# Products of probabilities and values of two sub-blocks issued back to back, every second step, in both attention mixers

## The chip, the cores and the metric

The kernel runs on one core of one Trainium2 chip. The time is that of the whole program on the device, in microseconds; a run's number here is the time of that one core. Of the kernel before, three runs were timed, and one further execution was taken with the hardware profiler.

## What is computed

Two layers of an encoder trunk on 512 tokens of 1024 channels. Each layer has one wide input projection that feeds two attention mixers, two gates, and then an output projection with a layer norm:

```python
u = x * (1.0 + scale) + shift                    # scale, shift, gate from c
aq, ak, av, az, bq, bk, bv, bz, gl = split(u @ w_in)
y_a = mixer_a(aq, ak, av, rel_table) * silu(az)  # 3 groups x 8 heads, windows, relative bias
y_b = mixer_b(bq, bk, bv, q_norm_g, k_norm_g) * silu(bz)   # 8 q heads, 2 kv heads, rms norm, rope
merged = g_a * (y_a @ w_pa) + g_b * (y_b @ w_pb)
x = layer_norm(ALPHA * x + gate * (merged @ w_o))
...
# both mixers, block by block
logits = einsum('qe,ke->qk', q, k) * scale (+ bias, masked)
p = exp(logits - max)
o = einsum('qk,ke->qe', p, v) / sum(p)
```

The change touches the last of these lines, the product of probabilities and values, in both mixers, and only the moment at which it is issued.

## The kernel before, in words

The order of the work is written out by hand: each engine executes its instructions in the order in which the Python code emits them, and semaphores hold an instruction until what it reads is there, or until what it overwrites has been read. TensorE (PE), VectorE (DVE), ScalarE (ACT), GpSimd (POOL) and the DMA queue of SyncE (SP) each have one such order.

**Main and fill.** `weave` (L854) runs two generators against each other. The main one is attention: `mixer_b` and then `mixer_a` for each half of the heads. The fill is the wide projection, `half_chunks` and `z_chunks`, in units of 12 products with 512 columns or 24 with 256 (rows `b<-uh,wh`, `b<-ul,wh`, `b<-uh,wl` and `b<-wh,uh`, `b<-wl,uh`, `b<-wh,ul`: weights and activations are split into a high and a low part, three products for each). Every `yield 1` of the main lets 1.1 fill units through on average. After each unit, `tick` (L340) splits the next piece of weights (`wh` on ACT in L175, `wl` on DVE in L176) and, in layer 0 above all, adds up pieces of the adaLN projection on DVE (`ada_dve`, L281 and L283).

**A sub-block** is 128 queries of two heads and all their keys. `pipeline` (L668) takes them through four stages. `L(i)` makes the logits in the PSUM tile `L`, and the softmax on DVE and ACT leaves the probabilities in the tile `s` (mixer B: maximum L631, exponential L637, scaling by the inverse sum L641; mixer A: bias and maximum L731, exponential L738). `T(i)` transposes them on PE, eight transposes into the PSUM tile `T` (L663), and ACT copies them to `pt` (L665). `V(i)` is the product with the values: eight products, `pt` against 64 columns of values each, that alternate between the upper and lower 64 columns of the array. A row of the profile shows each as two, so that one `V(i)` is 16 records `b<-pt,g 128*64`; all other stationary operands in these stretches have 128 columns. `Q(i)` (mixer B only, L613) transposes the queries two steps ahead.

**One step** of `pipeline` emits `T(i)`, `Q(i+2)`, `L(i+1)`, then a fill slot, then `V(i)`, then another fill slot. There are 16 steps in mixer B and 8 in each half of mixer A, for two layers 64 steps in all. In mixer B, DVE copies the result of each `V(i)` out of PSUM (L655). In mixer A two sub-blocks share one PSUM bank, and ACT copies it out after the second (L773).

**PSUM banks.** `B1` (L60, `Slots`) hands out four banks of one kind, `b`, first freed, first used, to the fill, `Q`, `V` and the sums of the adaLN projection (`ada_sum`, L296: one product with a tile of ones, read by DVE in L301 or L306). A bank counts as free when the code that reads it has been emitted; on the chip the next writer waits for that reader.

Of the kernel before, what the change touches and what calls it, by code (L numbers as in the profile page):

```python
# [38 lines left out]
def trunk_kernel(ctx, tc, x, c, rel_table, ln_g, ln_b, w_ada, b_ada, w_in, b_gate,  # L39
# [565 lines left out]
    def mixer_b(st, ys):  # L605
# [41 lines left out]
        def V(i):  # L647
# [8 lines left out]
            B1.put(o)  # L656

        yield from pipeline(len(subs), Q, L, T, V, lambda i: True, st["more"])

    def transpose_p(p):  # L660
# [7 lines left out]
    def pipeline(n, Q, L, T, V, need, more=()):  # L668
        if Q:
            Q(0)  # L670
            if n > 1:
                Q(1)
        yield 1
        while not need(0):
            yield "need"
        L(0)
        for _ in range(3 if Q else 2):
            yield 1
        for i in range(n):
            T(i)  # L680
            if Q and i + 2 < n:
                Q(i + 2)
            if i + 1 < n:
                while not need(i + 1):
                    yield "need"
                L(i + 1)
            yield 1
            V(i)
            if more:
                more.popleft()()  # L690
            yield 1
# [5 lines left out]
    def mixer_a(st, hf, ys, more=()):  # L697
# [90 lines left out]
        def need(i):  # L788
            k, pr, pp = subs[i]
            return all(("k", g, hf, pr) in st for g in ((1, 2) if k else (0,)))  # L790

        yield from pipeline(len(subs), None, L, T, V, need, more)
        for h in range(4):
            G.put(st.pop(("b0", hf, h)))
# [603 lines left out]
```

## Time and profile before

| what | value |
|---|---|
| median of three runs | 1199.09 us (1197.3 to 1199.76) |
| profiled execution, its own time | 1199.13 us |
| its span in the profile | 1197.0 us, so 2.1 us lie around it |
| mean granted clock of TensorE | 0.995 of full speed |
| busy share of PE, DVE, ACT, POOL | 97%, 56%, 44%, 5% |
| stretches with attention and fill | about 87 to 412 us (layer 0) and 665 to 988 us (layer 1) |

An engine's busy time counts each moment in which at least one of its instructions runs. Products on PE are pipelined: a record of 0.39 us may start every 0.23 us, so the distance from one start to the next tells what a product costs, not its length.

### The profile page before, as it was taken

The page shows a single profiled execution, that of the slowest core. Times are in us where ns is not written, and L with a number is a line of the kernel's source. Part 1 is how long each engine was busy: PE and PEld are TensorE (multiplying, and loading weights), DVE is VectorE, ACT ScalarE, POOL GpSimd, SP SyncE. Part 2 cuts the span into 40 slices and gives each one's busy share as a digit, 9 for nine tenths or more (in the row PEclk, how much of TensorE's full clock was granted, in tenths as well). Part 3 has the DMA queues.
Part 4 walks back from the last instruction along what each step waited for, and adds up shares of the span by engine and source line. Part 5 has one row for each costly group of instructions (what it writes and reads, how often), then busy time and mean ns, then how long its engine had stood idle before and what let it go on. Part 6 is the DMA issues. An engine that isn't in the chain of part 4 may idle for free.

```text
span 1197.0 us, 19187 instructions
## 1 busy us (share of the span) xinstructions
PE 1163.0 (97%) x7491; PEld 998.2 (83%) x7491; DVE 675.4 (56%) x1582; ACT 531.1 (44%) x1112; POOL 54.0 (5%) x85
## 2 busy tenths in 40 slices
PE   7899999999999999999989999999999999999996
PEld 6888888888887787888989888888878778888896
DVE  6776766655455365336755667664333533843477
ACT  2364544444554454323275545544554553533320
POOL 0021000001000000000002001000000000000000
PEclk9999999999999999999999999999999999999998
DMA  9935433546343243334522326335232223323331
GB/s 280 294 116 150 123 109 117 150 133 185 103 128 120 59 129 96 90 104 150 170 71 71 114 91 182 112 107 167 83 114 85 88 73 114 116 88 106 123 107 71
DMA packets 161314, 146.31 MB, mean 122 GB/s; under 512 B 8942, under 2 KB 149078, under 8 KB 161224
## 3 DMA queue, kind: packets, MB, share of 16 engines
q1 hardware_dynamic: 159176, 139.71, 38.5%
q0 software_dynamic: 2048, 5.38, 1.9%
q8 instruction: 59, 0.97, 0.3%
q14 instruction: 31, 0.25, 0.1%
HBM read 134.87 MB, written 8.62 MB: 120 GB/s over the span
## 4 chain that ended last, share of the span: by engine, by line
PE 88%; DVE 6%; ACT 2%; DMA 1%; issue 1%; SPq 1%; POOL 0%; DVEq 0%; ACTq 0%
PE b L90 75%; PE L L90 6%; PE T L663 5%; DVE acc L283 1%; PE T L90 1%; DMA raw<-in_w_ada_dram 1%; PE b L613 1%; DVE wl L176 1%; ACT g L948 0%; DMA s<-in_w_in_dram 0%; SPq L999 0%; DVE g L1252 0%; DVE g L1258 0%; ACT g L1271 0%; DVE wl L1023 0%
## 5 line engine op out<-in xcount | busy, mean ns | idle before, releaser
L176 DVE TENSOR_TENSOR wl<-raw,wh 128x512 fp32r<-128x512 f32 x304 | 205.1, 687 | 286.1 <-ACT wh L175 286.1
L90 PE MATMUL b<-uh,wh 128*128 128x512 f32 x768 | 308.4, 402 | 0.6 <-ACT g L423 0.6
L90 PE MATMUL b<-uh,wl 128*128 128x512 f32 x768 | 299.5, 390 | 1.7 <-DVE wl L176 1.7
L90 PE MATMUL b<-ul,wh 128*128 128x512 f32 x768 | 300.0, 391 | 0.0
L175 ACT ACTIVATE wh<-raw 128x512 fp32r<-128x512 f32 x304 | 179.9, 622 | 32.7 <-issue 24.8
L90 PEld LDWEIGHTS b<-uh,wh 128*128 128x128 f32 x768 | 144.0, 188 | 43.6 <-issue 12.0
L90 PEld LDWEIGHTS b<-uh,wl 128*128 128x128 f32 x768 | 144.2, 188 | 33.8 <-DVE wl L176 2.5
L90 PEld LDWEIGHTS b<-ul,wh 128*128 128x128 f32 x768 | 144.3, 188 | 27.6
L90 PE MATMUL b<-wh,uh 128*128 128x256 f32 x416 | 120.8, 290 | 0.0
L90 PE MATMUL b<-wl,uh 128*128 128x256 f32 x416 | 117.7, 283 | 0.0
L90 PE MATMUL b<-wh,ul 128*128 128x256 f32 x416 | 117.6, 283 | 0.0
L665 ACT ACTIVATE pt<-T 128x1024 f32<-128x1024 f32 x64 | 65.4, 1022 | 73.3 <-PE T L663 70.3
L738 ACT ACTIVATE s<-s,ast 128x256 f32<-128x256 f32 x128 | 63.5, 497 | 68.3 <-DVE ast L733 62.9
L283 DVE SCALAR_TENSOR_TENSOR acc<-raw,sc,acc 128x256 f32<-128x256 f32 x168 | 81.3, 484 | 8.4 <-DMA raw<-in_w_ada_dram 3.2
L90 PEld LDWEIGHTS b<-wh,uh 128*128 128x128 f32 x416 | 79.5, 191 | 4.8 <-issue 3.6
L90 PEld LDWEIGHTS b<-wl,uh 128*128 128x128 f32 x416 | 79.5, 191 | 0.8 <-DVE wl L176 0.2
L90 PEld LDWEIGHTS b<-wh,ul 128*128 128x128 f32 x416 | 79.4, 191 | 0.0
L90 PE MATMUL b<-g,wh 128*128 128x512 f32 x256 | 79.2, 391 | 0.0
L637 ACT ACTIVATE s<-L,bst,qn 128x512 f32<-128x512 f32 x64 | 49.2, 773 | 65.9 <-DVE bst L634 65.9
L90 PE MATMUL b<-wh,g 128*128 128x256 f32 x384 | 71.4, 284 | 0.7 <-DVE g L1191 0.5
L90 PE MATMUL b<-pt,g 128*64 128x128 f32 x1024 | 70.0, 279 | 0.0
L90 PEld LDWEIGHTS b<-pt,g 128*64 128x64 f32 x1024 | 54.6, 136 | 17.7 <-issue 13.7
(177 smaller groups left out, 1615.5 us busy)
## 6 DMA issues: line engine op xcount, KB each, us to landing
raw<-in_w_in_dram SPq DMA_DIRECT2D x126, 512.0 KB, 4.1
raw<-in_w_ada_dram SPq DMA_DIRECT2D x96, 256.0 KB, 3.9
raw<-in_w_o_dram SPq DMA_DIRECT2D x16, 512.0 KB
g<-in_x_dram SPq DMA_DIRECT2D x16, 256.0 KB, 5.5
vph<-g SPq DMA_DIRECT2D x16, 256.0 KB, 2.1
g<-vph SPq DMA_DIRECT2D x16, 256.0 KB, 6.0
g<-frow SPq DMA_DIRECT2D x32, 128.0 KB, 3.1
raw<-in_w_pa_dram SPq DMA_DIRECT2D x8, 512.0 KB, 3.5
```

Source lines behind the costliest of these rows:

```text
L90: pe.matmul(o, l, r, start=start, stop=stop, skip_group_check=True)
L175: act.activation(hi[:, d], raw[:, s], AF.Copy)
L176: dve.tensor_sub(lo[:, d], raw[:, s], hi[:, d].bitcast(F32))
L283: dve.scalar_tensor_tensor(a, raw[:, k], col, a, op0=MUL, op1=ADD)
L613: pe.transpose(o[:, 128 * e:128 * e + 128], qd[:, 2 * (hp % 2) + e], idn)
L637: act.activation(p[:, 512 * e:512 * e + 512], lg[:, 512 * e:512 * e + 512], AF.Exp, scale=f[:, e:e + 1], bias=sm[:, 0, e:e + 1], accum_out ...
L663: pe.transpose(t[:, 128 * j:128 * j + 128], p[:, 128 * j:128 * j + 128], idn)
L665: act.activation(pt, t, AF.Copy)
L738: act.activation(p4[:, e, b], p4[:, e, b], AF.Exp, bias=sm[:, e, b:b + 1], accum_out=s_t[:, rb, e, 1:2])
```

## The change

In `pipeline` the call `V(i)` becomes a pair on odd steps; even steps have none.

```diff
             yield 1
-            V(i)
+            if i % 2:
+                V(i - 1)
+                V(i)
             if more:
                 more.popleft()()
             yield 1
```

All numbers of steps are even, so every `V` is still issued. On PE 32 of the 64 `V` are emitted one step later, directly ahead of the next one; every other PE instruction keeps its place among the rest. On DVE the 16 copies L655 of even sub-blocks move behind with them. The orders of ACT, POOL and SP are the same, row by row. Two tiles `pt` exist before and after, and the pair uses both.

The TensorE order of layer 0, mixer B, steps 6 and 7, before (`T_`, `s_` and `pt_` belong to one sub-block each, `uh,wh` rows stand for a fill unit, `acc,ones` is the sum of a gate piece; the names' numbers count tiles, not banks):

```order
L663 MATMUL T_1642<-idn,s_1582 128x128 x8
L613 MATMUL b_1653<-idn,g_1434 128x128 x2
L90 MATMUL L_1659<-g_842,qst_1571 128x512 x4
L90 MATMUL b_1673<-uh,wh_1518 128x512
...
L90 MATMUL b_1714<-pt_1651,g_720 64x128 x8
L90 MATMUL b_1733<-uh,wh_1518 128x512
...
L663 MATMUL T_1748<-idn,s_1667 128x128 x8
...
L90 MATMUL b_1793<-acc_1634,ones 128x256
L90 MATMUL b_1801<-pt_1757,g_720 64x128 x8
L90 MATMUL b_1811<-wh_1686,uh 128x256
```

The same place on TensorE with the change:

```order
L663 MATMUL T_1642<-idn,s_1572 128x128 x8
L613 MATMUL b_1653<-idn,g_1434 128x128 x2
L90 MATMUL L_1659<-g_842,qst_1561 128x512 x4
L90 MATMUL b_1673<-uh,wh_1518 128x512
...
L90 MATMUL b_1723<-uh,wh_1518 128x512
...
L663 MATMUL T_1738<-idn,s_1667 128x128 x8
...
L90 MATMUL b_1783<-acc_1634,ones 128x256
L90 MATMUL b_1791<-pt_1651,g_720 64x128 x8
L90 MATMUL b_1801<-pt_1747,g_720 64x128 x8
L90 MATMUL b_1811<-wh_1686,uh 128x256
```

The product with `pt_1651` has moved from between two fill units to a place between the gate sum and the product with the next `pt`. With it the banks are dealt out differently: before, the fill tile `b_1811` came into a bank that `Q` had used, and the gate sum's bank went to a later `Q`. Now the two `V` take the two banks that are free ahead of it, and `b_1811` gets the bank of the gate sum `b_1783`.

On VectorE, the stretch behind the scaling L641 of step 7's logits, before:

```order
L641 TENSOR_SCALAR s_1773<-s_1773,bst_1770 128x512 x2
L306 TENSOR_TENSOR gate_631<-b_1793,gate_631 128x256
L176 TENSOR_TENSOR wl_1687<-raw_1359,wh_1686 128x512
L655 COPY g_783<-b_1801 128x128
L176 TENSOR_TENSOR wl_1837<-raw_1555,wh_1836 128x512
```

And with the change:

```order
L641 TENSOR_SCALAR s_1763<-s_1763,bst_1760 128x512 x2
L306 TENSOR_TENSOR gate_631<-b_1783,gate_631 128x256
L176 TENSOR_TENSOR wl_1687<-raw_1349,wh_1686 128x512
L655 COPY g_782<-b_1791 128x128
L655 COPY g_783<-b_1801 128x128
L176 TENSOR_TENSOR wl_1837<-raw_1545,wh_1836 128x512
```

The copy for the even sub-block, `g_782`, which stood a step earlier, now stands next to the odd one; nothing else moved.

## Rows read from the trace of the kernel before

**Rows 1.** The page: span, busy time by engine, the chain that ended last.
```profile
span 1197.0 us, 19187 instructions
...
PE 1163.0 (97%) x7491; PEld 998.2 (83%) x7491; DVE 675.4 (56%) x1582; ACT 531.1 (44%) x1112; POOL 54.0 (5%) x85
...
PE 88%; DVE 6%; ACT 2%; DMA 1%; issue 1%; SPq 1%; POOL 0%; DVEq 0%; ACTq 0%
```

**Rows 2.** Windows of both attention stretches: span, busy us (count) by engine, clock.
```profile
87.00:412.00 325.00, 324.37 (x2254) 273.12 (x2253) 185.05 (x498) 161.15 (x367) 12.82 (x20) 1.00 0.43 126
665.00:988.00 323.00, 323.00 (x2243) 271.13 (x2242) 166.82 (x443) 162.64 (x371) 12.67 (x20) 1.00 0.37 111
```

**Rows 3.** Groups by line and shape: the V products of the whole span.
```profile
L90 PE MATMUL b<-pt,g 128*64 128x128 f32 x1024 | 70.0, 279 | 0.0
```

**Rows 4.** Timeline of PE around one V, 512-column fill: start, length, instruction.
```profile
199.66 0.39 PE L90 MATMUL b<-uh,wl 128*128 128x512 f32 x1
...
202.38 0.39 PE L90 MATMUL b<-uh,wl 128*128 128x512 f32 x1
202.70 1.09 PE L90 MATMUL b<-pt,g 128*64 128x128 f32 x16
203.72 0.50 PE L90 MATMUL b<-uh,wh 128*128 128x512 f32 x1
...
204.52 0.40 PE L90 MATMUL b<-uh,wh 128*128 128x512 f32 x1
```

**Rows 5.** Timeline of PE around one V, 256-column fill.
```profile
220.12 0.28 PE L90 MATMUL b<-wh,ul 128*128 128x256 f32 x1
...
220.48 0.28 PE L90 MATMUL b<-wh,ul 128*128 128x256 f32 x1
220.69 1.09 PE L90 MATMUL b<-pt,g 128*64 128x128 f32 x16
...
222.18 0.28 PE L90 MATMUL b<-wh,uh 128*128 128x256 f32 x1
```

**Rows 6.** Timeline of PE inside the V of rows 4, in two pieces.
```profile
202.70 0.33 PE L90 MATMUL b<-pt,g 128*64 128x128 f32 x2
...
202.86 0.93 PE L90 MATMUL b<-pt,g 128*64 128x128 f32 x14
```

**Rows 7.** Timeline of PE: transposes T, then Q into another bank.
```profile
168.10 1.03 PE L663 MATMUL T<-idn,s 128*128 128x128 f32 x8
168.97 0.38 PE L613 MATMUL b<-idn,g 128*128 128x128 f32 x2
```

**Rows 8.** Timeline of PE at V(7) of layer 0, mixer B.
```profile
163.82 1.09 PE L90 MATMUL b<-pt,g 128*64 128x128 f32 x16
164.85 0.39 PE L90 MATMUL b<-wh,uh 128*128 128x256 f32 x1
```

**Rows 9.** Timeline of DVE at the same place; idle time would stand in brackets.
```profile
162.15 1.21 DVE L631 TENSOR_REDUCE bst<-L 128x2 f32<-128x1024 f32 x1
...
166.34 0.42 DVE L306 TENSOR_TENSOR gate<-b,gate 128x256 f32<-128x256 f32 x1
```

**Rows 10.** Timelines of PE and DVE, layer 0, mixer A: a weight piece and its use.
```profile
320.14 0.28 PE L90 MATMUL b<-wl,uh 128*128 128x256 f32 x1
...
318.75 0.69 DVE L176 TENSOR_TENSOR wl<-raw,wh 128x512 fp32r<-128x512 f32 x1 [2.93 <-ACT wh L175]
```

**Rows 11.** Timelines of PE and DVE before T(13), layer 0, mixer B.
```profile
215.67 1.07 PE L663 MATMUL T<-idn,s 128*128 128x128 f32 x8
...
208.53 2.04 DVE L283 SCALAR_TENSOR_TENSOR acc<-raw,sc,acc 128x256 f32<-128x256 f32 x4
...
214.22 0.88 DVE L641 TENSOR_SCALAR s<-s,bst 128x512 f32<-128x512 f32 x2
```

**Rows 12.** Timelines of PE and DVE before T(5), layer 1, mixer B.
```profile
714.88 1.04 PE L663 MATMUL T<-idn,s 128*128 128x128 f32 x8
...
712.09 0.88 DVE L641 TENSOR_SCALAR s<-s,bst 128x512 f32<-128x512 f32 x2
```

## The prediction

> **What bounds the kernel now.** I read the page first. PE is busy for 1163.0 of 1197.0 us, and 88% of the chain that ended last runs on PE [rows 1]; no other engine is above 56%. Then the two stretches with attention, by windows: PE is busy for 324.37 of 325 us and for 323.00 of 323 us, at a granted clock of 1.00 [rows 2]. So there is no waiting to remove here. A microsecond comes out only if PE's own stream becomes shorter, and whatever makes it shorter reaches the end unless a new wait eats it. The change removes no product: there are 1024 records of V, 64 V of 16, before and after [rows 3]. It can only gain by what lies at the seams, so the next view is the PE timeline around one V, read by starts.
>
> **What a V costs alone.** In a 512-column fill the products start every 0.2267 us: twelve of them from 199.66 to 202.38, 2.72 us [rows 4]. Across the V, from the fill product at 202.38 to the fourth one behind it at 204.52, 2.14 us pass; without the V the same four steps would take 0.907 us. One V costs PE 1.23 us. The reader can see where: the V starts 0.32 us behind the last fill product, the next fill product is 0.50 long, not 0.39, and the one after it comes 0.34 later instead of 0.23. Inside the V, the first two of the 16 records start at 202.70 and the next at 202.86; the last 14 take 0.93 us with the length of one record, 0.27, so seven pairs stand 0.66 us / 6 = 0.109 us apart [rows 6]. In 256-column fill it is the same: 220.12 to 220.48 gives 0.12 a product, and from 220.48 to 222.18 are 1.70 us where four steps need 0.48, so 1.22 us for the V [rows 5].
>
> **What it costs as the second of a pair.** Behind another V of the same shape, 16 more records are eight pair distances: 8 x 0.109 = 0.875 us. The rest, 1.233 - 0.875 = 0.358 us (0.345 in 256-column fill), is the price of going from 128-column stationary operands to 64-column ones and back, and the change pays it once for two V. Of the 32 V that move, 23 stand before 512-column and 9 before 256-column fill (counted in the order of the kernel before): 23 x 0.358 + 9 x 0.345 = 11.3 us. That two V can follow each other at 0.109 is the one price that no row shows. From below, nothing extra: T into one bank and then Q into another, two waits on other data, follow at 0.87 us for eight, 0.109 each, so a new bank and a new operand of the same shape cost nothing [rows 7]. From above, the second V starts afresh, with its first pair 0.154 instead of 0.109: 32 x 0.045 = 1.4 us less. I take nothing, since T and Q is the nearer case.
>
> The Trainium skill, TensorEngine Tiling (Array Packing), section Key Properties, says that a change of the tiling mode drains TensorE, and that a change of tile within a mode does not. By this rule the second V costs no drain and the sum is 11.3 us; by the upper bound above it would be 9.9 us. No run so far has two V side by side.
>
> **What the move makes earlier and later.** In an even step, everything on PE behind the missing V comes 1.23 us sooner, against the softmax and the weight pieces that hang on logits issued before it. Behind the pair, PE is only 0.355 us ahead of before. So a PE wait can arise only where the margin was under 1.23 us inside this window. I went through PE's waits on DVE and ACT there, with the partners' times left where they were unless they themselves follow PE. Three places fall short, all in layer 0, where DVE also does adaLN.
> - Bank of the gate sum, step 7 of mixer B. The fill behind V(7) began at 164.85 [rows 8]; with the pair it is due at 164.85 - 1.23 + 0.875 = 164.49. Its bank is now the gate sum's, which DVE reads in L306 from 166.34 to 166.76 [rows 9]. The reduction at 162.15 had no idle time before it: DVE is behind with the query rotation there, so an earlier PE doesn't move it; the removed copy L655 ahead of it gives some 0.2. The wait is about 166.56 - 164.49 = 2.0 us.
> - A weight piece in mixer A: PE read `wl` at 320.14, DVE had it at 319.44 [rows 10]. At 318.91 PE waits 0.55 us.
> - T(13): due at 215.67 - 1.23 = 214.44; its first four transposes need the first half of L641, done at 214.22 + 0.44 = 214.66 [rows 11]. With the wake-up, 0.3 us.
>
> Elsewhere the cover holds. In layer 1, T(5) had 714.88 - 712.97 = 1.9 us and keeps 0.7 [rows 12], and that is the usual case. If it went, each odd step would pay the shortfall. The copies L655 of even sub-blocks have no reader before the end of mixer B; the longer hold of `pt` costs nothing, as T(i+1) is issued only behind both V. No DMA and no row of ACT, POOL or SP changes its place, and the bank that mixer A held for a whole step is now held for the pair alone.
>
> **Sum.** -11.3 + 2.0 + 0.55 + 0.3 = -8.4 us. The profiled execution took 1199.13 us, 2.1 of them around the span of 1197.0, and it stands at the median of 1199.09. Predicted: 1190.7 us, 0.7% faster.
>
> **Rivals.**
> 1. *The waits dissolve.* DVE or ACT follows PE more closely than I assumed, or the bank is read sooner. Then the whole 11.3 is kept: 1187.8. For it: DVE is 57% busy in layer 0 (185.05 of 325 us). Against: no idle time before the row at 162.15.
> 2. *More waits.* Each pair now makes PE ask earlier, and in layer 0 DVE's backlog of 2.04 us of adaLN sums ahead of a softmax [rows 11] returns in several steps. Three more waits the size of the first would take 6 us: 1196.7 at the worst, 1193 to 1196 in the main.
> 3. *The softmax becomes the bound of odd steps.* If all odd steps were like T(13), 0.3 us short, 32 x 0.3 = 9.6 of the 11.3 us go: 1197.4, no change that can be told. Against: the margins of layer 1.
> 4. *The seam belongs to each V, not to the change of shape* (the slower side). If the array empties at the head of each group of 16, whatever stands before it, nothing is gained and the waits of 2.85 us remain: 1202. The point at which it decides: the second V must begin about 0.27 us later than its pair distance (11.3 - 2.85 = 8.45, over 32). For it: V is the only group on PE with such a seam in mixer B. Against: T then Q, above, and that the seam is paid on both sides, on leaving too.
>
> **Chances.** Forecast, 1188.5 to 1193: 0.70. Rival 1: 0.10. Rival 2: 0.10. Rival 3: 0.05. Rival 4: 0.05. A measurement of this kernel can tell about 0.2%, 2.4 us, from no change. So faster 0.90, the same 0.05, slower 0.05. The range runs from 1187.0, where all is kept, to 1195.5; the bound of 1.4 us on the second V and rival 2's main part lie in it.
>
> **What would show it.** In the trace after, rows `b<-pt,g` come as x32 with about 1.97 us from first start to last end, preceded by 0.32 and followed by 0.20 and a first fill product of 0.50, 32 times and not 64; two fill units in even steps follow each other at 0.227. A gap of some 2 us on PE, released by DVE L306, stands once near 163 us, and PE stays at clock 1.00. The prediction is wrong if a gap of 0.2 or more opens between the 16th and 17th record, if T waits for L641 or L738 in layer 1, or if PE's waits in layer 0 add up to much more than 3 us.

## The result and the profile after

The changed kernel took 1190.03 us (median; 1188.67 to 1191.2 in four runs) against 1199.12 for the kernel before on the same chip: ratio 0.9929, 95% interval 0.9915 to 0.9943. It is faster by 0.7%; 1190.7 was predicted.

The page of the kernel after: span, busy time by engine, the chain that ended last. They answer to [rows 1].

```profile
span 1189.1 us, 19164 instructions
...
PE 1152.1 (97%) x7491; PEld 1000.6 (84%) x7491; DVE 674.7 (57%) x1582; ACT 531.6 (45%) x1112; POOL 53.7 (5%) x85
...
PE 86%; DVE 7%; ACT 3%; DMA 2%; issue 1%; SPq 1%; POOL 0%; DVEq 0%; ACTq 0%
```

The same number of PE instructions is busy for 10.9 us less. PE is still the engine on which the time hangs.

The groups by line and shape, as [rows 3], the V products alone:

```profile
L90 PE MATMUL b<-pt,g 128*64 128x128 f32 x1024 | 63.0, 276 | 0.0
```

They cover 63.0 us where they covered 70.0. The count is 1024 as before, so the 7.0 us are head and tail of 32 groups, not products. The timeline of PE around a pair shows it. First a 512-column fill, to be held against [rows 4] (start, length, engine, instruction):

```profile
203.51 0.39 PE L90 MATMUL b<-uh,wl 128*128 128x512 f32 x1
203.83 1.97 PE L90 MATMUL b<-pt,g 128*64 128x128 f32 x32
205.72 0.50 PE L90 MATMUL b<-uh,wh 128*128 128x512 f32 x1
206.06 0.40 PE L90 MATMUL b<-ul,wh 128*128 128x512 f32 x1
```

Then a 256-column fill, to be held against [rows 5]:

```profile
221.66 0.28 PE L90 MATMUL b<-wh,ul 128*128 128x256 f32 x1
221.88 1.97 PE L90 MATMUL b<-pt,g 128*64 128x128 f32 x32
223.78 0.39 PE L90 MATMUL b<-wh,uh 128*128 128x256 f32 x1
224.00 0.28 PE L90 MATMUL b<-wl,uh 128*128 128x256 f32 x1
```

One row of 32 records stands where a row of 16 stood. It is 1.97 us long and the single V was 1.09 [rows 4, 5]: 0.88 us for 16 records, eight pairs of 0.110. Nothing opened between the 16th and the 17th record. The edges are those of a single V: 0.32 ahead (0.22 in 256-column fill), a first fill product of 0.50 (0.39), 0.34 to the next (0.22). All 32 pairs are rows of 32 records and 1.97 us.

Now the place where a wait was predicted, PE from the pair of step 7 on (layer 0, mixer B), as [rows 8]. A bracket gives the idle time ahead of an instruction and what ended it:

```profile
162.26 1.97 PE L90 MATMUL b<-pt,g 128*64 128x128 f32 x32
166.32 0.39 PE L90 MATMUL b<-wh,uh 128*128 128x256 f32 x1 [2.09 <-DVE gate L306]
166.54 0.28 PE L90 MATMUL b<-wl,uh 128*128 128x256 f32 x1
166.66 0.28 PE L90 MATMUL b<-wh,ul 128*128 128x256 f32 x1
...
168.12 0.41 PE L90 MATMUL b<-wh,uh 128*128 128x256 f32 x1
168.34 0.41 PE L90 MATMUL b<-wl,uh 128*128 128x256 f32 x1
168.55 0.41 PE L90 MATMUL b<-wh,ul 128*128 128x256 f32 x1
```

And DVE there, as [rows 9]:

```profile
161.67 1.21 DVE L631 TENSOR_REDUCE bst<-L 128x2 f32<-128x1024 f32 x1
...
164.85 0.17 DVE L639 RECIPROCAL bst<-bst 128x2 f32<-128x2 f32 x1 [1.78 <-ACT s L637]
165.05 0.88 DVE L641 TENSOR_SCALAR s<-s,bst 128x512 f32<-128x512 f32 x2
165.85 0.42 DVE L306 TENSOR_TENSOR gate<-b,gate 128x256 f32<-128x256 f32 x1
```

The first fill product waits 2.09 us until DVE has read the gate sum out of the bank. That is the wait foreseen, at its place, released by its line. L306 comes so late by DVE's order more than by DVE's work: it stands behind the softmax of the step, and there DVE itself is idle for 1.78 us until ACT has the exponential (L637). An earlier place for L306 on DVE was not tried. What was not foreseen is the end of the first fence: behind the wait the fill products stand 0.21 us apart (168.12, 168.34, 168.55), not 0.12. The windows say why (us; busy us and count of PE, PEld, DVE, ACT, POOL; granted clock; DMA share; GB/s):

```profile
164.00:166.40 2.40, 0.31 (x7) 0.08 (x1) 1.51 (x5) 2.34 (x6) 0.00 (x0) 1.00 0.00 0
166.40:168.00 1.60, 1.60 (x12) 1.60 (x13) 1.47 (x4) 0.00 (x0) 0.00 (x0) 0.84 0.01 2
168.00:172.00 4.00, 4.00 (x25) 4.00 (x25) 0.00 (x0) 0.07 (x1) 0.00 (x0) 0.64 0.44 130
```

The granted clock falls to 0.84 and 0.64 as means of these windows. In the trace it is one piece of 3.41 us, from 167.49 to 170.90, at half (1.2 GHz), and 1.00 on both sides. PE had run at 2.4 GHz up to the wait and for 1.2 us behind it. In the kernel before this place is at 1.00, as the same window of its trace shows:

```profile
168.00:172.00 4.00, 4.00 (x33) 3.82 (x32) 1.59 (x3) 1.30 (x2) 0.00 (x0) 1.00 0.44 131
```

The two small waits, PE and DVE at the weight piece of mixer A [rows 10] and at T(13) [rows 11], and T(5) of layer 1, where none was expected [rows 12]. PE:

```profile
320.24 0.38 PE L90 MATMUL b<-wl,uh 128*128 128x256 f32 x1 [0.34 <-DVE wl L176]
...
216.85 1.06 PE L663 MATMUL T<-idn,s 128*128 128x128 f32 x8 [0.32 <-DVE s L641]
...
711.09 1.03 PE L663 MATMUL T<-idn,s 128*128 128x128 f32 x8
```

DVE:

```profile
319.49 0.69 DVE L176 TENSOR_TENSOR wl<-raw,wh 128x512 fp32r<-128x512 f32 x1 [2.94 <-ACT wh L175]
...
216.22 0.88 DVE L641 TENSOR_SCALAR s<-s,bst 128x512 f32<-128x512 f32 x2
...
709.49 0.88 DVE L641 TENSOR_SCALAR s<-s,bst 128x512 f32<-128x512 f32 x2
```

In layer 1, T(5) begins 0.72 us behind the end of L641 (709.49 + 0.88 = 710.37), where 0.7 was predicted. Both attention stretches by windows, as [rows 2]:

```profile
87.00:412.00 325.00, 321.64 (x2257) 275.54 (x2256) 185.29 (x500) 161.84 (x368) 12.84 (x20) 0.99 0.43 127
...
665.00:988.00 323.00, 323.00 (x2263) 277.00 (x2262) 166.71 (x442) 162.94 (x370) 12.68 (x20) 1.00 0.38 113
```

Layer 1 has no PE wait at all; layer 0 lacks 3.4 us of busy time, 0.6 of them already before the change [rows 2].

The balance can be read by holding the start of the same PE instruction in both traces side by side. In layer 1 (from 665 to 990 us) the kernel after gains 6.1 us. In layer 0 (87 to 413, so that the last pair is in it) it gains 1.0. The half per layer of the 11.3 us of seams is 5.65, so in layer 0 some 4.7 us are eaten: 2.16 at the bank, 0.61 at the weight piece, 0.46 at T(13) (steps of the difference at these three places, idle time and slower restart together), and 1.2 between 166 and 180 us, the half clock. Some 0.35 more is missing at three V of mixer A, which in the kernel before stood behind a sum of adaLN pieces (`b<-ones,acc`, ahead of 299.98, 347.85 and 366.27 us): leaving these V out gave back 1.1 us and not 1.23, for fill right behind such a sum has a first product of 0.49 and 0.32 to the next too. The 0.4 us that layer 1 gained above 5.65 came in steps of under 0.06 that were not followed. The rest of the 7.9 us by which the trace is shorter is not the change's: 0.7 lost ahead of 30 us, where both kernels do the same, and 1.5 won near 622 us. There the profiled run of the kernel before has a half-clock piece of 3.41 us behind waits at the layer boundary, and the run after has none.

### The profile page after: what moved, and what is told of

It reads as the page before. It is cut to its first block, busy times and chain, and to the rows that moved or that the text cites. A ratio compares the mean times of both kernels' runs of the same rounds, so it can differ in the third digit from the quotient of the medians.

```text
span 1189.1 us, 19164 instructions
## 1 busy us (share of the span) xinstructions
PE 1152.1 (97%) x7491; PEld 1000.6 (84%) x7491; DVE 674.7 (57%) x1582; ACT 531.6 (45%) x1112; POOL 53.7 (5%) x85
## 4 chain that ended last, share of the span: by engine, by line
PE 86%; DVE 7%; ACT 3%; DMA 2%; issue 1%; SPq 1%; POOL 0%; DVEq 0%; ACTq 0%
PE b L90 73%; PE L L90 6%; PE T L663 5%; DVE acc L283 1%; DMA raw<-in_w_ada_dram 1%; PE T L90 1%; DVE wl L176 1%; PE b L613 1%; SPq L1001 0%; ACT g L950 0%; DMA g<-in_x_dram 0%; DMA s<-in_w_in_dram 0%; DVE g L1254 0%; DVE g L1260 0%; ACT wh L175 0%
## 5 line engine op out<-in xcount | busy, mean ns | idle before, releaser
L175 ACT ACTIVATE wh<-raw 128x512 fp32r<-128x512 f32 x304 | 179.9, 622 | 32.7 <-issue 24.8
L283 DVE SCALAR_TENSOR_TENSOR acc<-raw,sc,acc 128x256 f32<-128x256 f32 x168 | 81.3, 484 | 7.6 <-DMA raw<-in_w_ada_dram 2.4
L637 ACT ACTIVATE s<-L,bst,qn 128x512 f32<-128x512 f32 x64 | 49.2, 773 | 69.6 <-DVE bst L634 69.6
L663 PE MATMUL T<-idn,s 128*128 128x128 f32 x512 | 66.5, 273 | 0.3 <-DVE s L641 0.3
L663 PEld LDWEIGHTS T<-idn,s 128*128 128x128 f32 x512 | 59.1, 141 | 6.4 <-ACT wh L175 0.7
```

What stands on the lines that cost most here:

```text
L175: act.activation(hi[:, d], raw[:, s], AF.Copy)
L283: dve.scalar_tensor_tensor(a, raw[:, k], col, a, op0=MUL, op1=ADD)
L637: act.activation(p[:, 512 * e:512 * e + 512], lg[:, 512 * e:512 * e + 512], AF.Exp, scale=f[:, e:e + 1], bias=sm[:, 0, e:e + 1], accum_out ...
L663: pe.transpose(t[:, 128 * j:128 * j + 128], p[:, 128 * j:128 * j + 128], idn)
```

## Experiments

All times are medians; ratios are to the kernel before in the same series (1198.04, 1197.78, 1197.96 and 1197.85 us).

**The pairs once more, as the base of the series.**

> The changed kernel itself, as the partner of the others. My account: 32 seams of 0.35 us saved, 11.3 us, less a wait of 2.1 us on the gate sum's bank, less some 1.1 us of two smaller waits, and in executions where TensorE's clock drops to half behind that wait, about 1.4 us more. So times at two levels, about 1188.8 and 1191, ratio to before near 0.993.

1190.58 us, ratio 0.9931 (0.9919 to 0.9943), from 1189.2 to 1190.97 without two clear levels. The wait for L306 is there with 2.10 us, and again a half-clock piece of 3.41 us, from 166.15. So neither is of one execution alone; but the piece does not come in each. The run of 1188.67 us in the first series had a mean granted clock of 0.997 over 1186.9 us, which leaves at most 8.3 us at half clock, and the piece at the end of the span takes 5.7 to 8.7 us of that in the profiles: a further 3.41 us has no room. No profile shows whether that run had the wait.

**The gate sum one step later, with pairs and with single V.** The gate sum of the pieces concerned leaves its step, so that the fill behind the pair takes another bank:

```diff
-            later(2, lambda: ada_sum(l, g, a))
+            later(3 if g >= 8 else 2, lambda: ada_sum(l, g, a))
```

> The changed kernel, with the sums of gate pieces (ada_sum, four in each layer) issued one fill unit later, so that a fill unit behind a pair of V no longer gets the bank of a gate sum that VectorE has not read. If the wait on that bank and the clock drop behind it are what is missing from the 11.3 us: the wait of 2.1 us and the half-clock stretch near 167 us are gone, all executions lie at about 1187 (3 to 3.5 us under the executions with the drop, 2 us under those without), ratio to before near 0.990. Rival, that the wait is only hidden time that comes back at the next softmax: no change against the pair kernel, 1189 to 1191, and the later transposes T(8) or T(9) wait as long.

> The kernel before, with the same later gate sums and nothing else. If the later sum is of use only because the pair had taken the free banks: no change, 1199 plus or minus 1. If gate sums cost the kernel before too: 2 us or more faster.

With pairs 1188.21 us, ratio 0.9917 (0.9903 to 0.9930): 2.4 us less than the pairs alone, by medians whose intervals overlap; the traces show the place. With single V 1198.01, ratio 0.9998 (0.9989 to 1.0007): nothing. So the later sum has no worth of its own; it only takes away what the pairs had brought in. The same windows of the pairs with the later sum:

```profile
164.00:166.40 2.40, 2.25 (x19) 2.05 (x18) 1.54 (x4) 2.32 (x6) 0.00 (x0) 1.00 0.00 0
166.40:168.00 1.60, 1.42 (x10) 1.31 (x11) 0.61 (x4) 0.00 (x0) 0.00 (x0) 1.00 0.04 9
168.00:172.00 4.00, 4.00 (x32) 3.82 (x31) 2.66 (x5) 1.30 (x2) 0.00 (x0) 1.00 0.43 128
```

No wait for L306, none at T(8) behind it either, and the clock is 1.00 throughout; from 17.35 to 1177.88 us this trace has no half-clock piece. Between 160 and 180 us the pairs lose 3.0 us against the kernel before, this version gains 0.05. That is more than the 2.1 us of idle time: in these profiles the half clock goes with the wait. The 1187 us expected were missed by 1.2: this version has two waits that the pairs alone do not have, for L641 at 118.94 us and for `wl` at 166.58, and each costs 0.3 to 0.5 us by the starts.

**Pairs in one mixer only.** `Q` is given in mixer B alone. Mixer A alone has the edit below, mixer B alone has `not Q` in its place:

```diff
-            if i % 2:
+            if Q:
+                V(i)
+            elif i % 2:
                 V(i - 1)
                 V(i)
```

> Pairs in mixer A alone, 16 of the 32. By the seams: 16 x 0.35 = 5.7 us less the 0.55 us wait on a weight piece, so about 1194, ratio 0.9957. Rival, that mixer A gains as well from the PSUM bank that it no longer holds for a whole step: more than 7 us, under 1192, with PE waits on banks of the kernel before that are gone.

> Pairs in mixer B alone, single V in mixer A. My theory (0.36 us saved per pair, less a bank wait of 2.1 us behind the pair of V(6) and V(7), 0.45 us ahead of T(13), and about 1.3 us of half clock behind the bank wait): 16 x 0.36 = 5.8, less 3.9, leaves about 1.9 us, 1196 us, ratio 0.998. Rival, that the gains of the mixers simply add to the whole (1198.0 to 1190.6, of which mixer A alone gave 4.0): 3.4 us, 1194.6, ratio 0.997. Rival, that the bank wait is not tied to the pairs of mixer B: no L306 wait in the profile and 1192.5 us.

Mixer A alone: 1194.04 us, ratio 0.9956 (0.9942 to 0.9969), as the seams give it; the bank that it no longer holds shows no gain. Mixer B alone: 1196.29, ratio 0.9986 (0.9977 to 0.9995). By the starts of the same instructions A gains 2.0 us in layer 0 and 3.2 in layer 1, B loses 1.1 in layer 0 and gains 2.9 in layer 1: together 7.0, and the whole change has 7.1 by the same reading. So the parts add. The sum of the medians, 4.0 + 1.5 = 5.5 against 7.5, falls short of it, within intervals of some 1.5 us each; my rival of 3.4 us for B had been worked out from such medians and was no better than they are. The theory's 1196 us was met. Mixer B alone has the bank wait in full and the half clock behind it:

```profile
165.96 0.39 PE L90 MATMUL b<-wh,uh 128*128 128x256 f32 x1 [2.09 <-DVE gate L306]
```

```profile
164.00:168.00 4.00, 2.04 (x11) 2.04 (x12) 2.98 (x8) 1.98 (x5) 0.00 (x0) 0.81 0.03 10
168.00:172.00 4.00, 4.00 (x27) 3.91 (x26) 0.00 (x0) 0.43 (x1) 0.00 (x0) 0.76 0.41 122
```

But for the weight piece of mixer A and the three V behind sums, all the loss stands in layer 0 of mixer B.

**What makes the seam: the shape or the data type?** V differs from fill in two ways: its stationary operand has 64 columns, not 128, and its operands are float32. T is float32 too, but has 128 columns. So the pair was put directly ahead of T:

```diff
-            if i % 2:
-                V(i - 1)
-                V(i)
             if more:
                 more.popleft()()
             yield 1
+            if i % 2:
+                V(i - 1)
+                V(i)
```

> Each pair is issued directly ahead of T(i+1), whose products are float32 and 128 columns wide, in place of ahead of a fill unit. If the seam goes with the 64-column shape (my theory), leaving V towards T costs as much as leaving it towards fill: the row of T starts about 0.2 us behind the last V record, each pair still saves 0.36 us, and the time is that of the pairs, 1190 us, give or take what the waits move. If the seam goes with the change of data type (V and T are both float32, fill is not), the exit seam of 32 pairs vanishes: about 0.2 us x 32 = 6 to 7 us less, 1184 us. A third case: T, right behind V, waits for a softmax or a bank; then PE waits by T appear and the time is longer than 1190.

1189.36 us, ratio 0.9933 (0.9919 to 0.9947). PE around one of the 26 pairs that are followed by T:

```profile
292.28 0.39 PE L90 MATMUL b<-uh,wl 128*128 128x512 f32 x1
292.60 1.97 PE L90 MATMUL b<-pt,g 128*64 128x128 f32 x32
294.50 1.09 PE L663 MATMUL T<-idn,s 128*128 128x128 f32 x8
```

From the pair's start to T are 1.90 us, just what it is to a fill product (203.83 to 205.72, above). The way out costs the same, so the seam goes with the change between V's products and those on 128 x 128 operands, and the type alone doesn't explain it. Only the first distance behind the seam is cheaper: eight transposes take 1.09 instead of 1.03 us [rows 7], 0.06 us lost, against 0.11 lost in fill (0.34 for 0.23). That leaves some 0.05 us per pair.

Rows of the kernel before narrow it (PE, layer 1: between fill stand one product with a 32-column operand, a T, and logits of mixer A with 64 rows):

```profile
925.17 0.39 PE L90 MATMUL b<-uh,wl 128*128 128x512 f32 x1
925.40 0.27 PE L819 MATMUL b<-idn,ft 128*32 128x128 f32 x1
925.51 1.03 PE L663 MATMUL T<-idn,s 128*128 128x128 f32 x8
926.47 1.26 PE L90 MATMUL L<-g,g 64*128 64x128 f32 x16
927.66 0.50 PE L90 MATMUL b<-uh,wh 128*128 128x512 f32 x1
928.00 0.39 PE L90 MATMUL b<-ul,wh 128*128 128x512 f32 x1
```

Fill to the 32-column product takes 0.23 us and that product to T 0.11, the plain distances. So fewer columns alone make no seam. The logits have one like V: T to them takes 0.96 us where eight distances of 0.109 make 0.87, and behind them come a first fill product of 0.50 and 0.34 to the next. What V and these logits share is that their products use 64 of the 128 partitions, the lower and the upper half by turns (of the output in V, of the operands in the logits). Whether the half makes the seam or the turns do, no run tells.

The wait for L306 is gone in this version, for the bank is handed out otherwise, but two others stand there: 1.40 us for `wh` (ACT L175) and 0.66 for `wl`, with a half-clock piece of 3.41 us from 168.14. The next run asked whose these are.

**Both edits together.**

> Pairs directly ahead of T, with the gate sum issued later. From the last runs: leaving towards T costs about 0.05 us less per pair than leaving towards fill (exit 203 ns and 165 against 110 ns, in place of 203 and 337 against 227), some 28 pairs, 1.4 us; and the later sum takes the bank of the gate sum away from the fill in step 7. If the waits of 1.4 us (wh) and 0.66 us (wl) at 165 us are the weight pieces' own, behind the sum on ACT and DVE, the later sum removes them and the half clock behind them: 1188.2 less 1.4, about 1187, ratio 0.991. Rival: with the pair moved behind the second fill unit, PE asks for the pieces 1.97 us sooner whatever the sum does; then the waits of 2 us and the half clock stay, and it is 1189.4 as without the later sum.

1191.01 us, ratio 0.9940 (0.9927 to 0.9954): no gain, and the rival was right on the waits and the clock; its 1189.4 us lies in the interval, 1189.2 to 1192.4. PE at the place:

```profile
165.64 0.38 PE L90 MATMUL b<-wh,uh 128*128 128x256 f32 x1 [1.80 <-ACT wh L175]
166.37 0.39 PE L90 MATMUL b<-wl,uh 128*128 128x256 f32 x1 [0.34 <-DVE wl L176]
...
167.59 3.43 PE L90 MATMUL b<-pt,g 128*64 128x128 f32 x32
170.95 1.24 PE L663 MATMUL T<-idn,s 128*128 128x128 f32 x8
```

With the pair behind the fill unit, PE asks for the next weight piece about 2 us sooner than ACT has rounded it, whatever the gate sum does. The half-clock piece (from 167.89) now falls on the pair: 3.43 us in place of 1.97.

**The same, but step 7 left ahead of the fill.** The condition at the new place gets `and i != 7`, and step 7 keeps its pair at the old one.

> Pairs directly ahead of T with the later gate sum, but the pair of step 7 stands ahead of the fill unit, as in the version of 1188.2 us. Theory: the two waits on weight pieces at 165 us and the half clock behind them came from the fill unit that stood in the pair's place; without them PE waits no longer on wh L175, no half-clock stretch stands near 168 us, and the cheaper exit towards T (about 0.05 us for each of some 23 pairs, 1.2 us) is left: 1187.0, ratio 0.991. Rival: the pieces come late in some other step instead, and the time is 1189 or more.

1188.39 us, ratio 0.9920 (0.9906 to 0.9933). Of the theory the first half held: no wait for `wh`, and no half clock near 168 us. The 1.2 us below 1188.2 did not show. By the starts of the same instructions this version gains on the one with the later sum 0.7 us between 180 and 600 us and 0.7 between 640 and 1100, the cheaper exits. It loses 0.7 between 87 and 180 us, in small steps that I did not follow, and 1.5 between 618 and 640, where its profiled run has a half-clock piece at the layer boundary (from 620.11) and the other has none. Whether more runs would tell the two versions apart stays open.

**Runs of four in mixer A, and their control.** If the seam is paid per group, four V in a row should save again. Four `pt` tiles are needed, and their room comes from the tiles for raw weights, 3 in place of 5; the control has this change alone, on the version with the later sum.

```diff
-        RAW = 5
+        RAW = 3
```

```diff
-            if i % 2:
-                V(i - 1)
-                V(i)
+            if i % 2 and (Q or i % 4 == 3):
+                for j in range(i - 1 if Q else i - 3, i + 1):
+                    V(j)
```

> Control for the runs of four: the pairs with the gate sum issued later, with 3 raw weight tiles in place of 5. If the depth of the weight prefetch isn't used up, the time is that of the pairs with the later sum, 1188.2, ratio 0.992. If fewer raw tiles delay the pieces of the weights, PE waits for wl or wh grow: each of the four wl waits of about 0.6 us would be longer, 1190 us or more.

> The control with runs of four V in mixer A (every fourth step), pairs in mixer B. Mixer A then has 8 seams where the pairs have 16, and 32 single V had 32. Theory: 8 x 0.36 = 2.9 us less than the control, 1185.3 against 1188.2, as long as the softmax keeps up: in three steps of four everything on PE is 1.23 to 3.7 us earlier than with single V, where the transposes of mixer A had about 3 us of room. Rival: the room is used up, PE waits for L738 or L641 ahead of T in each fourth step, 0.4 us or more eight times, and the gain is gone: 1188 us or more.

Control 1193.51 us, ratio 0.9965 (0.9953 to 0.9978); fours 1192.46, ratio 0.9955 (0.9943 to 0.9968). The control's expectation by theory was wrong: the depth of the prefetch is worth 5.3 us. Its rival had the size but not the place, for no `wl` wait is longer. Most of it stands far from attention, at the start, where PE waits 9.6 us for adaLN sums (L283) ahead of 87 us, against 4.5 with five raw tiles; why they come later was not followed. Two of these waits:

```profile
45.77 0.61 PE L90 MATMUL b<-ones,acc 128*128 128x1 f32 x4 [0.87 <-DVE acc L283]
...
53.96 0.61 PE L90 MATMUL b<-ones,acc 128*128 128x1 f32 x4 [2.74 <-DVE acc L283]
```

In the runs of four the rows are as hoped:

```profile
285.67 0.39 PE L90 MATMUL b<-uh,wl 128*128 128x512 f32 x1
285.99 3.71 PE L90 MATMUL b<-pt,g 128*64 128x128 f32 x64
289.63 0.50 PE L90 MATMUL b<-uh,wh 128*128 128x512 f32 x1
```

3.71 - 1.97 = 1.74 us for 32 more records, 0.109 a pair, with the same edges. 2.9 us were expected. By the starts of the same instructions the eight runs gain 1.4 us on the control in layer 1 (four times 0.35) and 0.95 in layer 0, where a weight piece costs 0.4. The softmax of mixer A kept up. The medians differ by 1.05 us, which their intervals don't tell from these 2.35, nor from nothing. As the room for it costs more than it brings, the fastest version measured is the pair with the later sum, 1188.2 us.

## Why the prediction came out

**The seam.** The largest term was right in place and size: 0.358 us per pair, worked out from single V, is what each pair saves (0.36 between the missing V, -1.23, and the pair, +0.87) at 29 of the 32; the three behind sums saved some 0.24. The price that no row showed, V behind V, is the pair distance and no more; my bound of 1.4 us from above (1.6 by the 0.16 that a first pair takes in [rows 6]) was not touched. Layer 1, where nothing waits, gained 6.1 us against 5.65. The Trainium skill, TensorEngine Tiling (Array Packing), section Key Properties, says that a change of tiling mode drains TensorE and a change of tile does not. The traces agree: 1.97 us for 32 records and 3.71 for 64, and an exit of the same length towards T and towards fill; the price is in the rows, a drain itself is not. What the prediction named as the cause, stationary operands of 64 columns in place of 128, is too simple: the 32-column product has no seam, and the 64-row logits of mixer A have one. That did not touch the sum, since V is entered and left the same way in every pair.

**The waits.** The bank of the gate sum cost 2.16 us (2.0 predicted), the weight piece 0.61 (0.55), T(13) 0.46 (0.3). All three stood where they were read off, and no fourth came. The later sum showed the first one's cause, since it went with the bank. That DVE is late there because it is "behind with the query rotation" is half of it; the 1.78 us for which it waits on ACT ahead of L639 are the other.

**The missed term.** "PE stays at clock 1.00" was wrong. I had costed the 2.0 us wait at its length; in each of the three profiles that have it, 3.41 us at half clock came behind, worth some 1.2 us more. I had no row of such a wait in the middle of attention, and did not look at what the clock had done behind waits elsewhere, though the kernel before has a half-clock piece at its layer boundary.

**Why the number was good all the same.** The sum with this term is -7.2 and not -8.4 us, and the traces give -7.1 where both kernels are alike otherwise. The first series gave -9.1, the second -7.5, so the median of a few runs moves by more than the error, and the half-clock piece at the layer boundary, worth 1.5 us, was present in some executions and not in others. That 1190.7 lies within 0.7 us of the measured median is luck in part.

**The rivals.** That the seam belongs to each V (1202) is refuted by the rows of 32 and 64. That the waits dissolve (1187.8) did not happen; the later sum took the largest away by hand and came to 1188.2. That more waits come (1193 to 1196) is refuted by layer 0, which has the three and no fourth. That the softmax bounds the odd steps (1197.4) is refuted by layer 1, which has no wait, and by T(5), which kept the 0.7 us that was worked out; even runs of four in mixer A found no such bound.

## What to carry to other kernels

Where an engine is busy throughout, look for what its instructions cost at their edges: a small group of another kind pays for the change each time, so two side by side cost less than two apart (here 2.1 us against 2.46), and the price is readable as the distance across the group less the distances within. Regrouping also deals the banks out anew, so follow which tile the next product lands on and who still reads there; moving that reader's producer by a step was worth a third of the change. And cost a wait on TensorE together with what the clock does behind it.

## What the hardware showed that I had not expected

In three of three profiles a wait of 2.1 us on a TensorE that had been at 2.4 GHz was followed by 3.41 us at 1.2 GHz, which began 0.4 to 1.2 us behind the wait's end (166.15 behind 165.71, and 167.49 behind 166.32), not with it. Two waits close together, 1.40 and 0.66 us, or 1.80 and 0.34, were followed by the same piece of 3.41. At half clock 256-column products stand 0.21 us apart instead of 0.12, and a pair of V takes 3.43 us instead of 1.97. In the two versions whose waits here were 0.33 us (the pairs with the later sum, and the exception of step 7) no such piece stands near 168 us; in the runs of four, with waits of 0.33 and then 1.17 us around 170, none either. At the layer boundary, with the same 6 us of waits in four pieces, the half-clock piece comes in four of the twelve profiles (622.92 in the kernel before, 621.82 with mixer A alone) and is absent in the others (both profiles of the pairs); what decides it there the runs do not show. Nor did it come behind the 2.1 us wait in every execution, if the run of 1188.67 us had that wait.
